# The second gate of a transformer layer: multiplied into the weights w2, or into the products

## The chip, the cores and the metric

The kernel runs on one core of a Trainium2 chip. The core has a matrix engine (PE, with its weight loads as PEld), a vector engine (DVE), a scalar engine (ACT), a general engine (POOL) and a queue (SP) that issues the transfers. Each engine takes its instructions strictly in the order of the program; an instruction whose operands aren't ready holds everything behind it on the same engine. The metric is the device time of one execution in microseconds. Before the change three runs took 2816.18, 2817.00 and 2820.16 us, with a median of 2817.0 us.

## What is computed

One layer of a transformer over 2048 rows of 1024 numbers: a retention and an attention branch, their output projection, and a feed-forward part, with a norm at the end. The part that matters here is the end of the layer:

```python
mod = (c_act @ w_mod + b_mod)[:, None, :]
sh1, sc1, g1, sh2, sc2, g2 = jnp.split(mod, 6, axis=-1)
...
x = x + g1 * (jnp.concatenate([ret, att], axis=-1) @ w_out)
h2 = _modulate(_rmsnorm(x, norm2_g), sh2, sc2)
x = x + g2 * _sqrelu_mlp(h2, w_ff1, w_ff2)       # square(relu(h @ w1)) @ w2
return _rmsnorm(x, final_norm_g)
```

`g2` is one row of 1024 numbers, so that `g2 * (u @ w2)` equals `u @ (w2 * g2)`: the gate may be put into the product or into the columns of w2.

## The kernel before

**Products of seven.** Both feed-forward matrix products are done by a scheme of Strassen's kind: two by two blocks, seven products instead of eight. Every operand is written as a sum of two 16-bit parts (high and low); a product is 12 matmuls of 128x128 by 128x512 (high-high, high-low, low-high, for four blocks of 128). Seven linear forms are built of each operand (four additions on POOL for the sums, the high part on ACT, the low part on DVE), and the seven products are added together as they come out of PSUM (DVE, with one copy on ACT).

**The up half** computes `u = square(relu(h @ w1))` in 224 products. Blocks of 256 columns of w1 are taken one after the other (an item); the first eight and the last eight items serve one half of the rows, the eight between them both halves. A product's result is added into others on DVE (L1849), goes through ReLU on ACT (L1853) and a square on POOL (L1854), and is stored. Beside it, w2 is prepared for the down half: `w2_forms` makes the seven forms of one block of 256 rows of w2. `seven` fetches two tiles of 128x1024 (`b`), builds four sums on POOL (L1891, `bs`), scales and rounds to the high part on ACT (L1896) and makes the low part on DVE (L1902, `w2f`); the results are stored (L1942, `wf`). The sixteen blocks start 7 products apart, from the first item with two halves on.

**The down half** computes `u @ w2` in 32 pairs of row tiles of 7 products each: four rounds (a quarter of the 4096 each) of eight pairs. `down` issues the 12 matmuls, `down_out` takes the product out of PSUM (L2066, tiles `d`), and `gate` multiplies the finished quarter by the gate's row (L2094, on POOL, tile `g2b`) and adds it to the row of x (L2096, tile `y`, half on POOL, half on DVE). After rounds 0 to 2 the row is stored and read again in the next round (`x1`). In the last round ACT squares it for the norm (L2106), `ending` makes the root (L1338, L1339 on POOL) and the normed row (L2121 on DVE), which is stored. In the very last pair DVE does the gate and the addition for the second half of the columns.

**Scales.** So that 16-bit parts don't overflow, powers of two are worked out once, early (`ff_scales`): `scw` for w2, `scu` for u. What is left of these scales is multiplied into the gate's row there, which is stored as `gs`; `open_late` reads it back, spread over all partitions, as `g2b`.

**What sets the order.** Steps are numbered by product. Functions are put into lists with `on(step, phase, fn, ...)`; for each step the phases run in the order

```python
FPHASES = ("pe", "sum", "hi", "lo", "relu", "out", "square", "late", "dma")
```

and each function issues its instructions. So the program's order on an engine follows from step, phase and the order of the calls of `on`. Rings of buffers (`Ring`) hold several pairs at once: eight PSUM banks, nine tiles `w` for the 16-bit forms, eight rows `y`.

## Time and profile before

| | |
|---|---|
| median of the runs | 2817.0 us |
| profiled execution | 2816.61 us |
| its span (first to last instruction) | 2814.7 us |
| PE busy | 2668.3 us (95%) |
| DVE busy | 2190.4 us (78%) |
| POOL busy | 1933.2 us (69%) |
| ACT busy | 1465.0 us (52%) |
| granted clock of PE | 0.989 |
| up half, first to last matmul of it | 1630 to 2212 us |
| down half | 2212.5 to 2794.8 us |

A row of the profile's groups reads: line of the kernel, engine, operation, what is written from what is read, shapes and number of instructions, then busy time and mean duration in ns, then the idle time of the engine just before these instructions with what ended it. In a table of stretches, each row gives the busy time of the engines between two moments. In a timeline, each row is start, duration, engine, line and operation, with the wait before it in brackets. Rows of one line or tile give least, median and greatest duration in ns. The ends of matmuls are modelled: they follow each other faster than the duration that each is given.

### The profile page before, as it was taken

The numbers are of one execution on the slowest core, as the hardware profiler recorded it, in microseconds if no ns is written. First come the engines' busy times: TensorE is split into PE (matmuls) and PEld (weight loads), VectorE is DVE, ScalarE is ACT, GpSimd is POOL, SyncE is SP. The second block draws the span as 40 slices with busy tenths as digits, with TensorE's granted clock in tenths as the row PEclk, the third lists the DMA queues.
The fourth block names the chain that finished last, engine by engine and source line by source line (L and its number), as shares of the span: only waits on it lengthen the run. The fifth ranks groups of instructions, "written<-read, shape, count | busy, mean of one in ns | idle before, by whom it ended". The sixth has DMA issues, their size and how long they took to land.

```text
span 2814.7 us, 46065 instructions
## 1 busy us (share of the span) xinstructions
PE 2668.3 (95%) x16756; PEld 1602.8 (57%) x16756; DVE 2190.4 (78%) x3126; ACT 1465.0 (52%) x2441; POOL 1933.2 (69%) x1499
## 2 busy tenths in 40 slices
PE   6998999997899999999999899999999999999996
PEld 3877788875566566555666544444444444444443
DVE  3678847777977787877877578898876688888898
ACT  2535443335777777777777745555544322222232
POOL 2527427434766668886766679988865688888887
PEclk9999999999999999999999999999999999999998
DMA  6776876855211223333121264777783757575543
GB/s 213 269 260 203 283 274 218 283 180 184 66 52 52 66 72 106 96 105 91 60 82 45 91 236 138 234 252 248 245 275 106 249 180 284 176 274 171 187 143 112
DMA packets 329778, 482.88 MB, mean 172 GB/s; under 512 B 81991, under 2 KB 192839, under 8 KB 325070
## 3 DMA queue, kind: packets, MB, share of 16 engines
q1 hardware_dynamic: 329166, 479.66, 51.7%
q8 instruction: 132, 2.16, 0.3%
q14 instruction: 96, 0.79, 0.1%
q10 hardware_dynamic: 384, 0.26, 0.0%
HBM read 327.64 MB, written 152.20 MB: 170 GB/s over the span
## 4 chain that ended last, share of the span: by engine, by line
PE 57%; DVE 6%; POOL 5%; issue 2%; DMA 2%; ACT 1%; SPq 0%; POOLq 0%; DVEq 0%; ACTq 0%
PE pu L1838 7%; PE pu L1839 7%; PE pu L1837 7%; PE pd L2056 5%; PE pd L2054 5%; PE pd L2055 5%; PE o L243 3%; PE st L210 3%; PE st L209 3%; PE mp L172 3%; PE o L242 2%; PE bank L1603 2%; PE bank L1605 2%; PE bank L1604 2%; POOL plo L226 1%
## 5 line engine op out<-in xcount | busy, mean ns | idle before, releaser
L185 DVE TENSOR_REDUCE nm<-mp 128x1 f32<-128x512 f32 (+1 forms) x576 | 390.1, 684 | 170.9 <-PE mp L172 144.7
L226 POOL TENSOR_TENSOR plo<-p,phi 128x1024 f16<-128x1024 f32 x160 | 354.1, 2214 | 175.3 <-ACT phi L219 148.0
L215 ACT ACTIVATE p<-st 128x512 f32<-128x512 f32 x576 | 338.5, 597 | 196.8 <-PE st L210 128.2
L2056 PE MATMUL pd<-w,uf 128*128 128x512 f16 x896 | 339.6, 379 | 1.2 <-DVE uf L2047 1.2
L1837 PE MATMUL pu<-hf,w1f 128*128 128x512 f16 x896 | 339.6, 379 | 0.0
L1838 PE MATMUL pu<-hf,w1f 128*128 128x512 f16 x896 | 339.6, 379 | 0.0
L1839 PE MATMUL pu<-hf,w1f 128*128 128x512 f16 x896 | 339.6, 379 | 0.0
L2054 PE MATMUL pd<-w,uf 128*128 128x512 f16 x896 | 339.6, 379 | 0.0
L2055 PE MATMUL pd<-w,uf 128*128 128x512 f16 x896 | 339.6, 379 | 0.0
L219 ACT ACTIVATE phi<-p 128x1024 f16<-128x1024 f32 x288 | 303.9, 1055 | 0.0
L1065 PE MATMUL pso<-whi,hlo_l 128*128 128x512 f32 (+1 forms) x768 | 288.5, 376 | 10.6 <-DVE hlo_l L492 10.5
L1063 PE MATMUL pso<-whi,hhi_l 128*128 128x512 f32 (+1 forms) x768 | 297.5, 387 | 0.8 <-ACT whi L512 0.8
L1064 PE MATMUL pso<-wlo,hhi_l 128*128 128x512 f32 (+1 forms) x768 | 286.8, 373 | 0.8 <-DVE wlo L516 0.8
L242 PE MATMUL o<-wv,plo 128*128 128x65 f16 x2304 | 234.7, 193 | 25.2 <-POOL plo L226 18.4
L228 DVE TENSOR_TENSOR plo<-p,phi 128x512 f16<-128x512 f32 x256 | 241.2, 943 | 19.5 <-ACT phi L219 14.4
L2094 POOL TENSOR_TENSOR d<-d,g2b 128x512 f32<-128x512 f32 x126 | 199.8, 1586 | 70.5 <-DVE d L2066 68.6
L242 PEld LDWEIGHTS <-plo 128*128 128x128 f16 x2304 | 206.3, 98 | 68.6 <-POOL plo L226 26.4
L243 PE MATMUL o<-wv,phi 128*128 128x129 f16 x2304 | 242.5, 220 | 0.0
L1854 POOL TENSOR_TENSOR r<-r 128x512 f32<-128x512 f32 x128 | 172.1, 1350 | 86.4 <-ACT r L1853 86.1
L209 PE MATMUL st<-qr,ks 128*128 128x512 f16 x576 | 220.6, 383 | 7.0 <-ACT p L215 6.6
L210 PE MATMUL st<-qr,ks 128*128 128x512 f16 x576 | 220.7, 383 | 0.4
L172 PE MATMUL mp<-ks,qr 128*128 128x512 f16 x512 | 196.8, 384 | 25.6 <-DVE nm L185 25.2
(330 smaller groups left out, 6249.1 us busy)
## 6 DMA issues: line engine op xcount, KB each, us to landing
wm<-in_w_ff SPq DMA_DIRECT2D x64, 512.0 KB, 6.9
u<-r SPq DMA_DIRECT2D x128, 256.0 KB, 4.6
ur<-u SPq DMA_DIRECT2D x128, 256.0 KB, 5.9
y<-x SPq DMA_DIRECT2D x64, 512.0 KB, 6.4
wst<-in_w_in SPq DMA_DIRECT2D x60, 512.0 KB, 6.8
wf<-w2f SPq DMA_DIRECT2D x112, 256.0 KB, 3.9
w<-wf SPq DMA_DIRECT2D x28, 1024.0 KB, 10.1
w1r<-in_w_ff SPq DMA_DIRECT2D x48, 512.0 KB, 5.3
```

The lines of the kernel that those rows point to most:

```text
L185: nc.vector.tensor_reduce(dst, src, axis=AX.X, op=ALU.max, negate=True)
L210: mm(ps, ks2[:, self.g, k], q[:, 1], start=False, stop=True)
L215: nc.scalar.activation(self.p[kt // 2][:, kt % 2], self.s.pop(kt), AF.Exp, scale=HD**-0.5)
L226: nc.gpsimd.tensor_tensor(lo, p, hi, op=ALU.subtract)
L242: mm(o[:, : HD + 1], lo[:, i, c], v[:, : HD + 1], start=False, stop=False)
L243: mm(o, hi[:, i, c], v[:, :VW], start=False, stop=last)
L1837: mm(pu[hf, i], whi, hi, start=k == 0, stop=False)
L1838: mm(pu[hf, i], whi, lo, start=False, stop=False)
L1839: mm(pu[hf, i], wlo, hi, start=False, stop=k == 3)
L2054: mm(ps, u[:, 0, b], w[:, b, 0], start=b == 0, stop=False)
L2055: mm(ps, u[:, 0, b], w[:, b, 1], start=False, stop=False)
L2056: mm(ps, u[:, 1, b], w[:, b, 0], start=False, stop=b == 3)
```

## The change

The gate is multiplied into w2 where its forms are made: each of the two fetched tiles of a block is multiplied in place by the gate's row, one tile on POOL two steps ahead of the block's first sum, the other on DVE one step ahead of it. Blocks start 8 products apart instead of 7, the fifteenth 18 after the fourteenth and the sixteenth 11 after that one. The scale of w2 takes the greatest value of the gate into account, and the row of the gate is used unscaled (no `gs`). What is left of the scales is a column `scy`.

In the down half a product is multiplied by `scy` and added in one instruction on DVE, either to a known sum (tiles `d`) or straight into the row `y`; POOL adds the known sums to the row. Multiplications by the gate are gone, and so is the special case of the last pair. The final norm's row is scaled once by the root of 1024, so that the two sums of squares are added in the same POOL instruction that adds epsilon. The row is stored two steps earlier, the ending begins three steps earlier.

```diff
+                gm = b[:, 8:9]
+                nc.vector.tensor_reduce(gm, x["g", 1], axis=AX.X, op=ALU.max, apply_absolute_value=True)
+                nc.vector.tensor_tensor(w2, w2, gm, op=ALU.mult)
...
-                g, t = x["g", 1], b[:, 8:9]
-                nc.vector.tensor_tensor(t, c, c, op=ALU.mult)
-                nc.vector.tensor_scalar_mul(t, t, 2.0**-24)
-                nc.vector.tensor_scalar(g, g, t, w2, op0=ALU.mult, op1=ALU.mult)
-                do(s + 5, "store", lambda: nc.sync.dma_start(gs_d.unsqueeze(0), g[:1]))
+                nc.vector.tensor_tensor(scy, c, c, op=ALU.mult)
+                nc.vector.scalar_tensor_tensor(scy, scy, 2.0**-24, w2, op0=ALU.mult, op1=ALU.mult)
...
-        nc.sync.dma_start(ff["g2"], gs_d.partition_broadcast(P))
+        nc.sync.dma_start(ff["g2"], gate_d[1].partition_broadcast(P))
...
+        def gated(g):
+            w, eng = x["raw", g], nc.vector if g else nc.gpsimd
+            eng.tensor_tensor(w, w, ff["g2"], op=ALU.mult)
...
             on(b0 - 5 + g, "dma", fetch, g)
+            if gate:
+                on(b0 - 2 + g, "lo" if g else "sum", gated, g)
...
+        on(20, "late", lambda: nc.scalar.activation(ff["fg"], ff["fg"], AF.Copy, scale=float(D) ** 0.5))
...
-            w2_forms(first1 + 1 + 7 * m, b)
+            w2_forms(first1 + 1 + (8 * m if m < 14 else 11 * m - 32), b)
...
+        def plus(to, x):
+            nc.vector.scalar_tensor_tensor(to, ps, scy, x, op0=ALU.mult, op1=ALU.add)
...
+        def known(k, g, n, x):
+            d = xs_[x]
+            on(at + k, "square", lambda: nc.gpsimd.tensor_tensor(y[g, n], y[g, n], d, op=ALU.add))
...
         elif i == 1:
-            gate(at, p, 0, 0, add("x"))
+            plus(y[0, 0], y[0, 0])
+            known(1, 0, 0, "x")
+            made(at + 1, p, 0, 0)
         elif i == 2:
-            xs_["u2"] = add("x")
+            plus(new("u2"), xs_["x"])
+            known(1, 0, 1, "u2")
         elif i == 3:
-            xs_["u3"] = add("u2")
+            plus(new("u3"), xs_["u2"])
+            known(1, 1, 1, "u3")
         elif i == 4:
-            gate(at, p, 1, 0, add("u3"))
+            plus(y[1, 0], y[1, 0])
+            known(0, 1, 0, "u3")
+            made(at + 1, p, 1, 0)
         elif i == 5:
-            gate(at, p, 1, 1, add("u3", xs_["u3"]))
-            add("u2", xs_["u2"])
+            plus(y[1, 1], y[1, 1])
+            plus(y[0, 1], y[0, 1])
+            made(at, p, 1, 1)
         elif i == 6:
-            gate(at, p, 0, 1, add("u2", xs_["u2"]))
+            plus(y[0, 1], y[0, 1])
+            made(at, p, 0, 1)
...
-        on(at + 1, "square", lambda: eng.tensor_tensor(c, c, ff["g2"][:, s], op=ALU.mult))
-        eng2 = nc.vector if n or fast else nc.gpsimd
-        on(at + 2, "lo" if eng2 is nc.vector else "square", lambda: eng2.tensor_tensor(y, y, c, op=ALU.add))
...
-                on(at + 4, "dma", lambda: nc.sync.dma_start(x1_d[tiles_of(p)[g]], ys.pop((p, g))))
+                on(at + 2, "dma", lambda: nc.sync.dma_start(x1_d[tiles_of(p)[g]], ys.pop((p, g))))
...
+        def root():
+            nc.gpsimd.tensor_scalar(v, ss[:, :1], ss[:, 1:], D * EPS, op0=ALU.add, op1=ALU.add)
+            nc.gpsimd.tensor_tensor(r, v, half[:, :1], op=ALU.pow)
```

The order on the engines shows it at three places. The first is POOL in the middle of the up half, around one block of w2 (`b` the fetched tiles, `bs` their sums, `w1s` the sums of w1, `r` the squares of the up products). Before:

```order
L1891 TENSOR_TENSOR bs_23826<-b_23724 128x512
L1854 TENSOR_TENSOR r_23788<-r_23788 128x512
L1891 TENSOR_TENSOR bs_23850<-b_23747,bs_23826 128x512
L1854 TENSOR_TENSOR r_23810<-r_23810 128x512
L1808 TENSOR_TENSOR w1s_23875<-w1r_23646,w1r_23648 128x512
L1891 TENSOR_TENSOR b_23724<-b_23747,b_23724 128x512
```

After:

```order
L1892 TENSOR_TENSOR b_24102<-b_24102,g2b_20946 128x1024
L1854 TENSOR_TENSOR r_24124<-r_24124 128x512
L1808 TENSOR_TENSOR w1s_24188<-w1r_23964,w1r_23966 128x512
L1854 TENSOR_TENSOR r_24147<-r_24147 128x512
L1896 TENSOR_TENSOR bs_24212<-b_24102 128x512
L1854 TENSOR_TENSOR r_24171<-r_24171 128x512
```

One instruction of 128x1024 on the gate's row (`g2b`) stands ahead of the block's first sum, with squares and a sum of w1 between them.

The second is POOL in the last round of the down half, about one pair (`us` and `ur` are the sums and parts of u for the next pair). Before:

```order
L2039 TENSOR_TENSOR us_30788<-ur_30700,ur_30702 128x512
L2094 TENSOR_TENSOR d_30670<-d_30670,g2b_20946 128x512
L2039 TENSOR_TENSOR us_30813<-us_30788,ur_30729 128x512
L2039 TENSOR_TENSOR ur_30700<-ur_30729,ur_30700 128x512
L2094 TENSOR_TENSOR d_30821<-d_30821,g2b_20946 128x512
L1338 TENSOR_SCALAR cv_e_30841<-ss_30794 128x1
L1339 TENSOR_TENSOR cy_e_30842<-cv_e_30841,half_65 128x1
L2096 TENSOR_TENSOR y_30727<-y_30727,d_30821 128x512
```

After:

```order
L2048 TENSOR_TENSOR us_30651<-ur_30561,ur_30563 128x512
L2134 TENSOR_SCALAR cv_e_30659<-ss_30555 128x1
L2135 TENSOR_TENSOR cy_e_30660<-cv_e_30659,half_65 128x1
L2048 TENSOR_TENSOR us_30678<-us_30651,ur_30588 128x512
L2048 TENSOR_TENSOR ur_30561<-ur_30588,ur_30561 128x512
L2083 TENSOR_TENSOR y_30586<-y_30586,d_30661 128x512
L2083 TENSOR_TENSOR y_30586<-y_30586,d_30702 128x512
L2048 TENSOR_TENSOR us_30678<-ur_30590,us_30678 128x512
```

The gate's multiplications are gone, the root (`cv_e`, `cy_e`) of the pair before stands ahead of the second sum, and the known sums `d` go straight into the row `y`.

The third is DVE at the end of the program, from the last low part on. Before:

```order
L2066 TENSOR_TENSOR d_31154<-pd_31138,d_31135 128x512
L2114 TENSOR_TENSOR ss_31132<-ss_31132 128x1
L2066 TENSOR_TENSOR d_31174<-pd_31156,d_31135 128x512
L2114 TENSOR_TENSOR ss_31068<-ss_31068 128x1
L2121 SCALAR_TENSOR_TENSOR y_30927<-y_30927,cy_e_31171,fgb_20948 128x1024
L2066 TENSOR_TENSOR d_31196<-pd_31179,d_31174 128x512
L2121 SCALAR_TENSOR_TENSOR y_30902<-y_30902,cy_e_31194,fgb_20948 128x1024
L2066 TENSOR_TENSOR d_31218<-pd_31201,d_31196 128x512
```

After:

```order
L2140 SCALAR_TENSOR_TENSOR y_30777<-y_30777,cy_e_30960,fgb_20948 128x1024
L2140 SCALAR_TENSOR_TENSOR y_30753<-y_30753,cy_e_30982,fgb_20948 128x1024
L2075 SCALAR_TENSOR_TENSOR y_30916<-pd_30987,scy_273,y_30916 128x512
L2075 SCALAR_TENSOR_TENSOR d_31015<-pd_31002,scy_273,d_30983 128x512
L2075 SCALAR_TENSOR_TENSOR d_31035<-pd_31019,scy_273,d_31015 128x512
L2075 SCALAR_TENSOR_TENSOR y_30936<-pd_31039,scy_273,y_30936 128x512
```

The norm of the pair before (the rows that write `y` from `cy_e`) stood on both sides of the addition for product 3 of the last pair (the third L2066 row) and now stands ahead of its first multiply-add.

More of the change, by code (lines that the diff above doesn't have):

```diff
@@ L1877, in store_u, with seven @@
         nc.sync.dma_start(dst, r.rearrange("p (q t) -> p q t", q=4))
-    def seven(b0, source, tiles, low, kinds, scale=None):
+    def seven(b0, source, tiles, low, kinds, scale=None, gate=None):
         x = {}
@@ L1944, in w2_forms @@
             scw,
+            True,
         )
@@ L2062, in down_out, with new @@
         ps = pu.pop(i)
-        def add(x, to=None):
-            to = to if to is not None else ff["r"].tile([P, 512], F32, "d")
-            nc.vector.tensor_tensor(to, ps, xs_[x], op=ALU.add)
-            return to
+        y = {(g, n): ys[p, g][:, n * 512 : (n + 1) * 512] for g in range(2) if (p, g) in ys for n in range(2)}
+        def plus(to, x):
+            nc.vector.scalar_tensor_tensor(to, ps, scy, x, op0=ALU.mult, op1=ALU.add)
+        def new(x):
+            xs_[x] = ff["r"].tile([P, 512], F32, "d")
+            return xs_[x]
@@ L2106, in square @@
             nc.scalar.activation(junk, y, AF.Square, accum_out=sums[p, g][:, n : n + 1])
[L2108 removed]
+        on(at + 1, "relu", square)
         if n == 1:
[L2110 removed]
+            on(at + 1, "relu", ending, at + 1, p, g)
     def ending(at, p, g):
         ss, y, t = sums.pop((p, g)), ys.pop((p, g)), tiles_of(p)[g]
[L2114 to L2118 removed]
+        v, r = (sm.tile([P, 1], F32, name=f"c{x}_e", tag=f"c{x}_e") for x in "vy")
+        def root():
+            nc.gpsimd.tensor_scalar(v, ss[:, :1], ss[:, 1:], D * EPS, op0=ALU.add, op1=ALU.add)
+            nc.gpsimd.tensor_tensor(r, v, half[:, :1], op=ALU.pow)
+        on(at, "square", root)
         def whole(c):
```

20 lines of the change are left out of this document (5 added, 15 removed).

## The prediction

> **What bounds the kernel now.** I read the table of busy time by stage first, with stretches cut at the borders of the two feed-forward halves: up (1630 to 2212 us) and down (from 2212.5 us).
>
> ```profile
> core 0: us, PE busy (x) PEld busy (x) DVE busy (x) ACT busy (x) POOL busy (x), PEclk, DMA share, GB/s
> 1690.00:1780.00 90.00, 90.00 (x419) 40.83 (x418) 77.09 (x84) 47.48 (x77) 90.00 (x62) 1.00 0.48 144
> 1953.70:1989.95 36.25, 36.25 (x169) 16.44 (x168) 31.48 (x36) 19.97 (x30) 29.27 (x20) 1.00 0.76 247
> ...
> 2212.50:2670.00 457.50, 457.50 (x2121) 207.42 (x2120) 377.78 (x402) 124.54 (x208) 395.35 (x253) 1.00 0.65 223
> 2670.00:2794.80 124.80, 123.54 (x570) 55.34 (x568) 117.81 (x124) 43.84 (x97) 108.52 (x83) 1.00 0.37 127
> 2794.80:2814.70 19.90, 0.00 (x0) 0.00 (x0) 14.19 (x20) 3.26 (x10) 9.76 (x12) 0.60 0.28 106
> ```
>
> PE has no idle time in either half until the last 125 us, and its clock is 1.00. So nothing that only relieves DVE or POOL can shorten these stretches. A product is 12 matmuls; 168 of them (14 products) take the 36.25 us of the second row, so a matmul goes out every 0.215 us and a product takes 2.59 us. What is left to win is the 19.90 us after the last matmul, and the 1.26 us that PE lacks in the row above. What is left to lose is PE's cover in the up half, where the change puts work.
>
> Then the timeline of the end, of PE, of DVE and of POOL, each alone:
>
> ```profile
> 2783.86 0.39 PE L2056 MATMUL pd<-w,uf 128*128 128x512 f16 x1 [0.53 <-DVE uf L2047]
> ...
> 2787.27 0.39 PE L2056 MATMUL pd<-w,uf 128*128 128x512 f16 x1 [0.64 <-DVE uf L2047]
> ```
>
> ```profile
> 2799.28 0.68 DVE L2066 TENSOR_TENSOR d<-pd,d 128x512 f32<-128x512 f32 x1
> 2800.08 1.28 DVE L2121 SCALAR_TENSOR_TENSOR y<-y,cy_e,fgb 128x1024 f32<-128x1024 f32 x1
> 2801.28 2.87 DVE L2066 TENSOR_TENSOR d<-pd,d 128x512 f32<-128x512 f32 x4
> ...
> 2806.56 0.69 DVE L2096 TENSOR_TENSOR y<-y,d 128x512 f32<-128x512 f32 x1
> ...
> 2810.13 1.42 DVE L2121 SCALAR_TENSOR_TENSOR y<-y,cy_e,fgb 128x512 f32<-128x512 f32 x2 [0.44 <-POOL cy_e L1339]
> ```
>
> ```profile
> 2807.41 0.19 POOL L1338 TENSOR_SCALAR cv_e<-ss 128x1 f32<-128x1 f32 x1 [2.76 <-DVE ss L2114]
> 2807.69 0.55 POOL L1339 TENSOR_TENSOR cy_e<-cv_e,half 128x1 f32<-128x1 f32 x1
> 2808.35 0.72 POOL L1338 TENSOR_SCALAR cv_e<-ss 128x1 f32<-128x1 f32 x1
> 2809.16 0.94 POOL L1339 TENSOR_TENSOR cy_e<-cv_e,half 128x1 f32<-128x1 f32 x1
> ```
>
> PE waits twice, 0.53 and 0.64 us, for a low part (uf) that DVE makes late; each wait hides another 0.38 - 0.215 us under the end that the matmul before it is given, so 1.5 us together. After the last matmul, at 2794.8, five additions out of PSUM (L2066) are still to come, the first of them for product 3 of the last pair of tiles, whose matmuls ended three products, 7.8 us, before that: it starts 12.3 us late. So DVE carries a backlog, and the end is this backlog and then the chain behind its last piece (gate, add, square, root, norm, store). A DVE that is 12 us late has cost PE 1.5 us: I use 10 to 12 us as the lag that the buffers absorb.
>
> **The change, part by part.** The rows of before that carry the prices:
>
> ```profile
> L2094 POOL TENSOR_TENSOR d<-d,g2b 128x512 f32<-128x512 f32 x126 | 199.8, 1586 | 70.5 <-DVE d L2066 68.6 <-DVE ss L2114 1.8
> L2096 DVE TENSOR_TENSOR y<-y,d 128x512 f32<-128x512 f32 x64 | 108.8, 1701 | 7.1 <-POOL d L2094 7.0
> L2096 POOL TENSOR_TENSOR y<-y,d 128x512 f32<-128x512 f32 x64 | 93.0, 1454 | 4.5
> ```
>
> ```profile
> L1610 DVE SCALAR_TENSOR_TENSOR xr<-bank,sco,xr x32: 734/749/752, 791.7 to 1635.7; 128x512 f32<-128x512 f32 x32
> ```
>
> ```profile
> b<-in_w_ff SPq DMA_DIRECT2D x32, 512.0 KB, 5.2
> ```
>
> *Down half, per pair of tiles (7 products, 18.1 us).* Removed are four gate multiplications (4 x 1.586 = 6.3 us) and two additions (2.9 us) on POOL, and two additions on DVE (3.4 us). Added are four additions on POOL, 1.26 us (alone, the fastest of L2094's kind) to 1.72 us each: 5.0 to 6.9 us. The seven additions from PSUM become multiply-adds; L1610 is the same form (PSUM, a column, a row), so 0.749 instead of 0.68 us, 0.5 us per pair. The first row of the stage gives 457.5 / 18.1 = 25.3 pairs, so 14.9 us of DVE and 15.6 us of POOL per pair before; after it DVE has 14.9 - 3.4 + 0.5 = 12.0 and POOL 15.6 - 9.2 + 5.0 to 6.9 = 11.4 to 13.3. All of this lies beside a PE that is already full: worth nothing by itself. In the last eight pairs, where the norm is added, DVE stands at 117.81 and POOL at 108.52 of 124.80 (17.1 and 15.7 us per pair) and work falls behind; the same subtraction leaves about 14 and 11.5 to 13.5 of 18.1. So the backlog goes, and with it the PE stalls: **-1.5 us**, if what gates PE next (POOL's sums, ACT's high parts) holds six products ahead as in the order. The norm loses its own small addition on DVE (ss) and runs a step or more earlier; the output stores move forward with it in SP's queue, past the reads of the next rows. Two waits are new. DVE's multiply-add for product 5 (and those of 5 and 6 into the first row) wait for POOL's additions of the known part: POOL gets to the one for product 5 after product 3 is out and has 5.2 us until product 5 ends, against at most 1.72 + 1.72 us for a sum ahead of it and itself. Behind that wait on DVE stand low parts that PE needs 5 products (13 us) later. And product 1 now needs its row of x, where before its first use was the add two steps later: fetched four steps (10.4 us) ahead, and a fetch of 512 KB, its size, lands in 5.2 us in the row above.
>
> *The end.* From the end of before's last addition, 2806.56 + 0.69 = 2807.25, to the end of the span at 2814.70 are 7.45 us: square on ACT, the ss addition, two POOL steps, two halves of the norm, their stores. Without the ss addition about 7.2. The last matmul is then followed by one multiply-add of 0.75 us and this chain: 0.05 + 0.75 + 7.2 = 8.0 us instead of 19.9: **-11.9 us**. Lower end 7.1, if POOL's two steps don't meet DVE (0.72 and 0.94 us there, 0.19 and 0.55 for the root before it: -0.9); upper end 9.4, if the norm of the other row (1.42 us) still stands ahead on DVE. I take 8.0, since the last rows of the order are the same.
>
> *The scales,* once, near 626 us.
>
> ```profile
> L914 DVE TENSOR_REDUCE fsb<-fg 128x1 f32<-128x1024 f32 x1 | 1.2, 1220 | 0.0
> ```
>
> A greatest value over the gate comes, of the same form as this row, and the scaling of that row of 1024 (L908) and its store go: between 0 (hidden, or the one for the other) and +1.2 us on DVE. I take **+0.5**, since two instructions over the same row stand against each other. The scaling of the final norm's row on ACT (1024 elements, once, with ACT half idle) and the column in ACT's copy are covered by PE.
>
> *Up half: the gate on w2.* Each of 16 blocks gets two multiplications of 128x1024, one on POOL, one on DVE, and blocks come 8 products apart instead of 7. Prices of the rows:
>
> ```profile
> L226 POOL TENSOR_TENSOR plo<-p,phi x160: 2114/2132/2692, 662.3 to 1607.4; 128x1024 f16<-128x1024 f32 x160
> ```
>
> ```profile
> L2121 DVE SCALAR_TENSOR_TENSOR y<-y,cy_e,fgb x18: 746/1272/2286, 2677.8 to 2810.8; 128x1024 f32<-128x1024 f32 x14, 128x512 f32<-128x512 f32 x4
> ```
>
> ```profile
> L1891 POOL TENSOR_TENSOR bs<-b,bs 128x512 f32<-128x512 f32 x4 | 5.5, 1384 | 2.5 <-DVE w2f L1902 1.9 <-DMA u<-r 0.6
> L1891 POOL TENSOR_TENSOR b<-b 128x512 f32<-128x512 f32 x2 | 3.4, 1720 | 0.0
> ```
>
> ```profile
> L1902 DVE SCALAR_TENSOR_TENSOR w2f<-b,scw,w2f 128x512 f16<-128x512 f32 x8 | 9.5, 1186 | 0.0
> L1849 DVE TENSOR_TENSOR r<-pu,r 128x512 f32<-128x512 f32 x14 | 9.4, 685 | 4.8 <-PE pu L1839 4.1 <-issue 0.6
> L1902 DVE SCALAR_TENSOR_TENSOR w2f<-bs,scw,w2f 128x512 f16<-128x512 f32 x7 | 9.4, 1347 | 0.0
> ```
>
> So 2.13 to 2.69 us on POOL and 1.27 to 2.29 us on DVE, the ends alone and meeting the other engine. The last two fences are of 1953.70 to 1989.95 us, two blocks in 14 products. POOL: 29.27 us, 12.3 of them w2 sums (5.5, 3.4, and two more of the kind at 3.4), so 17.0 for the rest, which follows the products. Over 16 products (41.4 us) that is 17.0 x 16/14 + 12.3 + 4.3 to 5.4 = 36.0 to 37.1 us, 87 to 90% (81% before). DVE: 31.48 us, the w2 low parts 18.9 less some 0.08 us of overlap each, 17.7 for 15 of them; the rest 13.8 grows to 15.8, 14 low parts are 16.5, the gates 2.5 to 4.6: 34.8 to 36.9 us, 84 to 89% (87% before). The wider spacing pays for the gates. Nothing of it is on PE's path as long as DVE and POOL are not later than those 10 us; 1690 to 1780 us, with POOL busy 90.00 of 90.00 us and PE too, shows that a full POOL is borne for 35 products. I cost it at **nothing**; its cover is PE's two halves of work, and if the engines overrun, each microsecond past 10 to 12 us of lag is one of PE. The gates also wait for the block's fetch, three steps (7.8 us) after its issue instead of five; it lands in 5.2 us, so they need not wait; a late one would hold POOL's squares and DVE's PSUM additions, who have the same 10 us. The last two blocks, at 175 and 186 of 220 steps, fall among products with one half each, where DVE and POOL had most room.
>
> *Sum:* -1.5 - 11.9 + 0.5 = **-12.9 us**. The profiled execution was 2816.6 us (span 2814.7, 1.9 around it), 0.4 below the median of 2817.0; against the median I forecast **2804.1 us**, 2801.5 to 2806 by the ends of the tail and the scatter of the runs.
>
> **A price for meeting engines.** How far POOL and DVE slow each other when both run from SBUF decides the up half:
>
> ```profile
> L2047 DVE TENSOR_TENSOR uf<-ur,uf x128: 670/681/1757, 2196.7 to 2786.5; 128x512 f16<-128x512 f32 x128
> ```
>
> ```profile
> 1966.36 1.72 POOL L1891 TENSOR_TENSOR bs<-b,bs 128x512 f32<-128x512 f32 x1
> 1968.04 1.72 POOL L1891 TENSOR_TENSOR b<-b 128x512 f32<-128x512 f32 x1
> ...
> 1978.73 1.04 POOL L1854 TENSOR_TENSOR r<-r 128x512 f32<-128x512 f32 x1 [4.14 <-ACT r L1853]
> 1979.73 1.27 POOL L1891 TENSOR_TENSOR bs<-b,bs 128x512 f32<-128x512 f32 x1
> ```
>
> Alone a square takes 1.04 and a sum 1.27 us; in a row against a busy DVE two sums come 1.68 us apart, 0.4 us more, less than the 0.67 us that a DVE low part needs alone. A strict taking of turns would add 0.67. The Trainium skill ("SBUF — State Buffer", Who interferes with whom) says that a DVE instruction with two SBUF inputs and a GpSimd instruction that reads SBUF lock each other out for the whole instruction, and that one with a single SBUF input doesn't contend. By that the multiply-adds from PSUM are harmless (L1610's 734 to 752 ns agree), and the up half would be overfull, the rival below; the trace shows 0.4 where the rule gives 0.67.
>
> **Rivals.**
> *Slower: strict turns in the up half.* Counting every POOL instruction and every two-input DVE instruction one after the other, a block of 8 products asks for 4.57 squares x 1.04 + 6.29 sums x 1.27 + 2.13 = 14.9 us of POOL and 11 x 0.67 + 1.2 = 8.6 of DVE, 23.5 of 20.7 us. Fourteen blocks fall 39 us behind; less 12 borne, PE loses 27 us: 2817 - 13 + 27 = 2831. It decides from 1.8 us of overrun per block. Against it: the same count of before is 18.8 of 18.1 us, yet DVE waited 4.1 us for PE in that stretch. 10%.
> *The turns as measured:* with 0.4 us per meeting a POOL instruction adds only its time alone less 0.27 us to DVE's 0.67 (0.77 for a square, 1.0 for a sum, 2.0 for the gate at 2.69 - 0.67): 3.5 + 6.3 + 2.0 + 8.6 = 20.4 of 20.7, just full. With 1 to 1.3 us more per block, fourteen blocks lag 14 to 18 us, and PE loses 2 to 8 us: 2806 to 2812. 12%.
> *The backlog stays.* If the product-5 wait makes DVE and POOL hand lateness to each other in the last pairs, PE's end stays and half of the tail with it: 2809 to 2817. 8%. For it speaks that DVE waited for POOL at L2096 already (7.0 us); against it, the 1.8 us of slack above (5.2 less 3.4).
>
> **Numbers.** The forecast has 70%. Times within 0.2% (5.6 us, about what a measurement of this kernel tells from no change) are 2811.4 to 2822.6. Faster: 70 + 12 + 1 = 83%; same 6%; slower 11%. The range of 8 in 10 runs from 2801 (shortest tail, and the scatter of the runs) to 2811.
>
> **What would show it.** Right: after the last matmul about 8 us instead of 19.9, with one multiply-add between it and the last square; no PE row with a wait for uf in the last pairs; DVE and POOL at about 12 us per pair in the down half, with the multiply-adds at 0.75 us; PE still at 100% from 1780 to 2070 us with DVE and POOL below 92%. Wrong: waits of PE for w1f or PSUM between 1780 and 2150 us, gates on POOL far over 2.7 us, or DVE waiting long for POOL's known part.

## The result, and the profile after

The changed kernel takes 2810.8 us (median of 13 runs, 2807.0 to 2816.5) against 2818.4 us of the kernel before in the same sessions (2816.2 to 2820.3): a ratio of 0.9975, 95% interval 0.9968 to 0.9983. It is faster by about 7.6 us, or a quarter of a per cent, where 12.9 us were forecast. The time lies above the forecast (2804.1) and above the 2801.5 to 2806 us given with it, at the upper end of the wider range (2801 to 2811).

The profiled execution of the changed kernel took 2814.1 us, 3.3 above the median, with a span of 2812.3 us. The first view to read is where its two halves lie: the row of the first of the up half's three matmul lines, with its first and last start. Before:

```profile
L1837 PE MATMUL pu<-hf,w1f x896: 379/379/379, 1630.1 to 2212.0; 128*128 128x512 f16 x180
```

After:

```profile
L1837 PE MATMUL pu<-hf,w1f x896: 376/379/379, 1633.0 to 2223.9; 128*128 128x512 f16 x180
```

The up half starts 2.9 us later. That is scatter and no effect of the change: the profiled executions of all eleven kernels of this study start it between 1627.6 and 1635.2 us. From its first to its last matmul the up half took 581.9 us before and takes 590.9 now, **9.0 us more**. From there to the end of the span it was 2814.7 - 2212.0 = 602.7 us and is 2812.3 - 2223.9 = 588.4, **14.3 us less**. The three add up: 2.9 + 9.0 - 14.3 = -2.4 us, the difference of the spans.

The stretches by stage, of the changed kernel, answer to the first table of the prediction (the last row lies behind the last matmul, which is now given an end at 2804.9):

```profile
core 0: us, PE busy (x) PEld busy (x) DVE busy (x) ACT busy (x) POOL busy (x), PEclk, DMA share, GB/s
1690.00:1780.00 90.00, 90.00 (x419) 40.83 (x418) 77.09 (x82) 49.64 (x81) 90.00 (x62) 1.00 0.49 146
1953.70:1989.95 36.25, 36.25 (x170) 16.41 (x169) 36.25 (x33) 17.49 (x29) 32.17 (x21) 1.00 0.60 197
...
2212.50:2670.00 457.50, 457.50 (x2121) 207.39 (x2120) 273.92 (x354) 125.36 (x208) 301.03 (x202) 1.00 0.63 224
2670.00:2794.80 124.80, 124.80 (x580) 56.57 (x579) 98.65 (x109) 50.73 (x107) 102.75 (x81) 1.00 0.45 152
2804.90:2812.30 7.40, 0.00 (x0) 0.00 (x0) 3.49 (x5) 0.72 (x2) 1.25 (x3) 0.70 0.38 142
```

In the down half DVE fell from 377.78 to 273.92 us and POOL from 395.35 to 301.03 of 457.5. PE lacks nothing in the last pairs (124.80 of 124.80, before 123.54), and 7.4 us instead of 19.9 follow the last matmul. In the up half DVE is now busy without a gap (36.25 of 36.25, before 31.48). The end on DVE, from its timeline:

```profile
2802.41 1.41 DVE L2075 SCALAR_TENSOR_TENSOR y<-pd,scy,y 128x512 f32<-128x512 f32 x2 [1.91 <-PE pd L2065]
2804.93 0.75 DVE L2075 SCALAR_TENSOR_TENSOR y<-pd,scy,y 128x512 f32<-128x512 f32 x1 [1.11 <-PE pd L2065]
2805.59 1.41 DVE L2140 SCALAR_TENSOR_TENSOR y<-y,cy_e,fgb 128x512 f32<-128x512 f32 x2
2807.85 1.41 DVE L2140 SCALAR_TENSOR_TENSOR y<-y,cy_e,fgb 128x512 f32<-128x512 f32 x2 [0.85 <-POOL cy_e L2135]
```

DVE waits for PE ahead of each multiply-add: no backlog is left, and one multiply-add stands behind the last matmul. The other row's norm (2805.59) still stands ahead of the last one, but it fills the gap while the last row is squared, and DVE waits another 0.85 us after it.

The loss lies in the up half. The waits of PE from 1660 to 2240 us, of which before had none:

```profile
PE pu L1839 <- DVE w1f L1819: 4.4, 8, 1.4
PE pu L1837 <- DVE r L1849: 1.8, 2, 1.6
```

PE waits for what DVE makes: low parts of w1, and the addition that frees a PSUM bank. These waits are 6.2 of the 9.0 us; the rest is later starts that the modelled ends of the matmuls hide, some 0.16 us at each wait, and gaps too small to be listed. Where they lie, two stretches of the changed kernel show (columns as above):

```profile
1780.00:2080.00 300.00, 298.17 (x1382) 134.99 (x1381) 289.59 (x275) 148.51 (x230) 264.02 (x165) 1.00 0.66 212
2080.00:2220.00 140.00, 135.35 (x619) 59.40 (x618) 127.35 (x134) 72.04 (x113) 115.33 (x77) 1.00 0.73 235
```

How late DVE is shows in two timelines. PE's last matmul of product 149 (products are numbered here from the fifth of the up half on), and DVE some 17 us later, when it gets to that product (the second of the two additions at 2051.35):

```profile
2034.54 0.38 PE L1839 MATMUL pu<-hf,w1f 128*128 128x512 f16 x1
```

```profile
2042.46 2.64 DVE L1907 SCALAR_TENSOR_TENSOR w2f<-b,scw,w2f 128x512 f16<-128x512 f32 x1
2045.02 1.27 DVE L1849 TENSOR_TENSOR r<-pu,r 128x512 f32<-128x512 f32 x2
2046.22 1.56 DVE L1819 SCALAR_TENSOR_TENSOR w1f<-w1s,sc,w1f 128x512 f16<-128x512 f32 x1
2047.70 1.52 DVE L1907 SCALAR_TENSOR_TENSOR w2f<-bs,scw,w2f 128x512 f16<-128x512 f32 x1
2049.15 2.28 DVE L1892 TENSOR_TENSOR b<-b,g2b 128x1024 f32<-128x1024 f32 x1
2051.35 1.28 DVE L1849 TENSOR_TENSOR r<-pu,r 128x512 f32<-128x512 f32 x2
```

DVE never waits here, and its instructions fall into two kinds: the additions out of PSUM (L1849) take 1.27 us for two in a row, 0.68 each, and everything that reads two operands from SBUF (L1907, L1819, L1892) takes 1.5 to 2.6 us. Measured in this way, from the end of a product to DVE's start on it, DVE's lag is 2.0 us at product 54, 10.9 at 102, 17.0 at 149: 15.0 us in 95 products, about 1.3 us per block of 8. A block therefore asks for about 20.7 + 1.3 = 22.0 us. The groups by shape between 1780 and 2080 us, before and after, show where it comes from. Before:

```profile
L1849 DVE TENSOR_TENSOR r<-pu,r 128x512 f32<-128x512 f32 x115 | 77.3, 683 | 31.0 <-PE pu L1839 22.1 <-DMA u<-r 5.3 <-issue 3.2
L1902 DVE SCALAR_TENSOR_TENSOR w2f<-b,scw,w2f 128x512 f16<-128x512 f32 x64 | 75.4, 1178 | 1.5 <-ACT w2f L1896 1.5
L1902 DVE SCALAR_TENSOR_TENSOR w2f<-bs,scw,w2f 128x512 f16<-128x512 f32 x48 | 66.6, 1387 | 0.0
L1819 DVE SCALAR_TENSOR_TENSOR w1f<-w1r,sc,w1f 128x512 f16<-128x512 f32 x25 | 31.7, 1268 | 0.8 <-ACT w1f L1813 0.8
L1819 DVE SCALAR_TENSOR_TENSOR w1f<-w1s,sc,w1f 128x512 f16<-128x512 f32 x35 | 30.9, 883 | 0.0
```

After:

```profile
L1854 POOL TENSOR_TENSOR r<-r 128x512 f32<-128x512 f32 x63 | 92.2, 1463 | 8.7 <-ACT r L1853 8.6
L1907 DVE SCALAR_TENSOR_TENSOR w2f<-b,scw,w2f 128x512 f16<-128x512 f32 x54 | 82.3, 1530 | 0.0
L1849 DVE TENSOR_TENSOR r<-pu,r 128x512 f32<-128x512 f32 x111 | 73.0, 677 | 4.3 <-DMA u<-r 4.3
L1907 DVE SCALAR_TENSOR_TENSOR w2f<-bs,scw,w2f 128x512 f16<-128x512 f32 x40 | 54.3, 1361 | 5.6 <-issue 2.8 <-ACT w2f L1901 2.8
L1819 DVE SCALAR_TENSOR_TENSOR w1f<-w1s,sc,w1f 128x512 f16<-128x512 f32 x32 | 37.2, 1162 | 0.0
L1892 POOL TENSOR_TENSOR b<-b,g2b 128x1024 f32<-128x1024 f32 x14 | 37.0, 2644 | 0.4 <-DMA b<-in_w_ff 0.4
L1819 DVE SCALAR_TENSOR_TENSOR w1f<-w1r,sc,w1f 128x512 f16<-128x512 f32 x24 | 34.1, 1421 | 0.0
L1892 DVE TENSOR_TENSOR b<-b,g2b 128x1024 f32<-128x1024 f32 x14 | 27.5, 1963 | 0.5 <-DMA b<-in_w_ff 0.5
```

The gates cost what was forecast (2.64 us on POOL, 1.96 on DVE) and hardly wait for their fetch (0.4 and 0.5 us in 300 us). But the low parts, the same instructions as before, went from 1178 to 1530 ns (of `b`), from 883 to 1162 and from 1268 to 1421 ns (of w1); only those of `bs` did not change (1387, 1361). Over all four kinds the mean rose from 1.19 to 1.39 us, some 30 us for the 150 of them in these 300 us.

What stretches a low part can be read from the same traces. Between 1640 and 2220 us of the changed kernel, 31 of the 274 low parts of w1 and w2 overlap with no instruction on POOL; each of these takes 0.73 to 0.75 us. The other 243 overlap with one and take 1.39 us on average, at most 2.88. Before, 56 and 217 low parts divide in the same way: at most 0.75 us, and 1.27 on average. The additions out of PSUM, with one operand from SBUF, take 0.68 us in both cases:

```profile
L1849 DVE TENSOR_TENSOR r<-pu,r x221: 671/677/693, 1643.1 to 2219.6; 128x512 f32<-128x512 f32 x111
L1907 DVE SCALAR_TENSOR_TENSOR w2f<-b,scw,w2f x64: 734/1523/2877, 1788.8 to 2167.0; 128x512 f16<-128x512 f32 x64
```

DVE no longer waits for PE anywhere in this stretch (22.1 us of such waits before).

### The profile page after: what moved, and what is told of

Read it like the earlier page. It is cut to its first block, busy times and chain, and to the rows that moved or that the text cites. A ratio compares the mean times of both kernels' runs of the same rounds, so it can differ in the third digit from the quotient of the medians.

```text
span 2812.3 us, 45879 instructions
## 1 busy us (share of the span) xinstructions
PE 2673.6 (95%) x16756; PEld 1605.7 (57%) x16756; DVE 2122.4 (75%) x3061; ACT 1463.5 (52%) x2442; POOL 1886.5 (67%) x1453
## 5 line engine op out<-in xcount | busy, mean ns | idle before, releaser
L226 POOL TENSOR_TENSOR plo<-p,phi 128x1024 f16<-128x1024 f32 x160 | 355.1, 2220 | 171.4 <-ACT phi L219 141.3
L1837 PE MATMUL pu<-hf,w1f 128*128 128x512 f16 x896 | 339.6, 379 | 1.8 <-DVE r L1849 1.8
L2083 POOL TENSOR_TENSOR y<-y,d 128x512 f32<-128x512 f32 x128 | 210.5, 1646 | 137.8 <-ACT uf L2052 90.8
L228 DVE TENSOR_TENSOR plo<-p,phi 128x512 f16<-128x512 f32 x256 | 239.1, 934 | 19.5 <-ACT phi L219 14.2
L243 PEld LDWEIGHTS <-phi 128*128 128x128 f16 x2304 | 205.4, 97 | 20.7
## 6 DMA issues: line engine op xcount, KB each, us to landing
w<-wf SPq DMA_DIRECT2D x28, 1024.0 KB, 10.8
```

The lines of the kernel that those rows point to most:

```text
L226: nc.gpsimd.tensor_tensor(lo, p, hi, op=ALU.subtract)
L243: mm(o, hi[:, i, c], v[:, :VW], start=False, stop=last)
L1837: mm(pu[hf, i], whi, hi, start=k == 0, stop=False)
```

## The experiments

**Theory.** POOL and DVE's instructions with two operands from SBUF hold each other up, so their times add, in full or in part: each new POOL instruction is paid once more, at least in part, on DVE. A block asks for more than its 20.7 us, DVE falls behind from block to block, and PE waits once the buffers are used up. **Rivals.** The own time of DVE (or of POOL) is what overflows; or the order of the waits around the gates makes single pieces late.

For each run the table gives the time, the ratio to before in the same session (2818.4 to 2818.8 us), the length of the up half from its first to its last matmul of L1837, and what DVE and POOL were busy of the 300 us from 1780 to 2080 us (the last four columns are of one profiled execution each).

| kernel | median us | ratio, 95% | up half us | last of it to end us | DVE | POOL |
|---|---|---|---|---|---|---|
| before | 2818.4 | | 581.9 | 602.7 | 263.7 | 243.9 |
| after | 2810.8 | 0.9975 (0.9968 to 0.9983) | 590.9 | 588.4 | 289.6 | 264.0 |
| down half alone | 2804.2 | 0.9945 (0.9933 to 0.9957) | 581.4 | 588.5 | 261.9 | 240.7 |
| both gates on DVE | 2804.7 | 0.9954 (0.9941 to 0.9966) | 584.5 | 588.4 | 295.2 | 233.4 |
| both gates on POOL | 2817.2 | 0.9994 (0.9985 to 1.0003) | 596.8 | 588.4 | 281.5 | 288.6 |
| all blocks 9 apart | 2810.1 | 0.9964 (0.9951 to 0.9978) | 586.9 | 588.4 | 283.5 | 266.1 |
| squares on ACT | 2802.0 | 0.9939 (0.9927 to 0.9952) | 581.0 | 588.4 | 247.6 | 163.9 |
| gates on DVE, 9 then 12 apart | 2803.1 | 0.9945 (0.9931 to 0.9958) | 581.1 | 588.4 | 282.2 | 227.9 |
| fetch and gates three steps earlier | 2817.6 | 0.9990 (0.9981 to 0.9999) | 593.8 | 588.4 | 288.9 | 264.7 |
| blocks 7 apart | 2828.9 | 1.0037 (1.0025 to 1.0048) | 607.6 | 588.4 | 292.4 | 273.4 |
| squares on ACT, blocks 7 apart | 2802.3 | 0.9944 (0.9924 to 0.9963) | 581.7 | 588.5 | 288.4 | 191.9 |

What comes after the up half is the same in all ten kernels that have the new down half, to 0.1 us. Everything that sets them apart happens in the up half.

**The down half alone.** The gates on w2 and their spacing are undone, so this kernel leaves the second gate out of its result:

```diff
-            if gate:
-                on(b0 - 2 + g, "lo" if g else "sum", gated, g)
...
-            w2_forms(first1 + 1 + (8 * m if m < 14 else 11 * m - 32), b)
+            w2_forms(first1 + 1 + 7 * m, b)
```

> The changed kernel without the two multiplications by the gate and with blocks of w2 7 products apart again, so that the up half is that of before and the down half and the end are those of the change; the second gate is left out of the result. All theories lay the missing half of the gain at the up half: PE then waits nowhere in the up half beyond its first products, the end takes 7.4 us as in the changed kernel, and the time is 2802 to 2804 us against 2818 before. If the down half itself is worth only half of what was forecast, it stays near 2811.

2804.2 us (2799.3 to 2805.6), at the upper edge of what was expected: 14.2 us below before, with an up half like that of before (581.4 us). So the change in the down half, its end and the scales is worth the whole forecast and a little more, and the gates on w2 take back 2810.8 - 2804.2 = 6.6 us of it.

**Both gates on DVE, both on POOL.** The two runs pull the rivals apart: one loads DVE more, the other relieves it.

```diff
-            w, eng = x["raw", g], nc.vector if g else nc.gpsimd
+            w, eng = x["raw", g], nc.vector
...
-                on(b0 - 2 + g, "lo" if g else "sum", gated, g)
+                on(b0 - 2 + g, "lo", gated, g)
```

The other kernel has `nc.gpsimd` and `"sum"` at the same places.

> Both gates of a block on DVE, otherwise the changed kernel. Theory (POOL and DVE take turns at what both need, so the sum of their times counts): a gate on DVE takes 1.2 us of the turns, on POOL 2.0 us, so a block asks for 0.8 us less; DVE falls behind by at most 0.5 us per block instead of 1.3, PE hardly waits, 2802 to 2805 us. First rival (DVE's own time is what is full, at 97%): DVE gets 1.2 to 2.1 us more per block, PE loses 17 to 29 us more, 2828 to 2840 us. Second rival (waits for the gates, by order, not load): about as the changed kernel, 2811 us.

> Both gates of a block on POOL, otherwise the changed kernel. Theory of turns: 0.8 us more per block, so about 12 us more lost by PE, 2820 to 2825 us. First rival (DVE's own time): DVE is relieved of 2.1 us per block, no PE waits, 2802 us. Second rival (order): about 2811 us.

Both gates on DVE, 1780 to 2080 us (columns as in the first table):

```profile
1780.00:2080.00 300.00, 300.00 (x1392) 136.01 (x1390) 295.24 (x295) 152.43 (x237) 233.40 (x156) 1.00 0.67 218
```

Both on POOL:

```profile
1780.00:2080.00 300.00, 293.98 (x1355) 132.30 (x1353) 281.45 (x254) 144.37 (x223) 288.63 (x174) 1.00 0.65 209
```

With DVE at 98% PE has no idle time; with DVE at 94% and POOL at 96% it loses 6 us here. The times are 2804.7 and 2817.2 us. DVE's own time is not what decides: the kernel that gives DVE more is the fastest of the three, and the one that relieves it the slowest. POOL's own time is not it either, as far as the waits show: in these 300 us of the changed kernel DVE has no wait for a result of POOL. 2804.7 us lies in the range that the theory gave; 2817.2 lies on the side expected but 2.8 us below the 2820 to 2825, so the second gate on POOL cost about half of the 12 us reckoned. A gate costs 1.77 us on DVE and 2.70 on POOL (its means in the two runs), and on POOL it also slows DVE. In the first run the lag still grew by about 0.8 us per block (2.7 us at product 54, 12.7 at 149), where at most 0.5 was expected; so my count of a block is too low there too.

**All blocks 9 apart.**

```diff
-            w2_forms(first1 + 1 + (8 * m if m < 14 else 11 * m - 32), b)
+            w2_forms(first1 + 1 + 9 * m, b)
```

> All sixteen blocks 9 products apart (the last starts two products later than in the changed kernel), gates as in the change. Theory of turns: a block's 21.5 us (22.9 with the 6.5% that the changed kernel measured above the count) fit into 23.3 us while products come in two halves, so the lag stays below 8 us up to product 164; the last three blocks then lie among products of one half, ask for 28.8 of 23.3 us and bring 16 us of lag, of which PE loses 2 to 4 us: 2804 to 2807 us. Rival (DVE's own time): the same direction, DVE busy below 95%. Rival (order of the waits): the spacing changes little, 2809 to 2811 us.

From 1780 to 2080 us and from there to 2220 us:

```profile
1780.00:2080.00 300.00, 300.00 (x1391) 135.99 (x1390) 283.49 (x278) 152.09 (x235) 266.14 (x169) 1.00 0.68 214
2080.00:2220.00 140.00, 135.38 (x623) 60.17 (x622) 129.63 (x133) 70.91 (x111) 113.80 (x75) 1.00 0.74 236
```

With 23.3 us per block the lag stays between 0 and 7 us from product 53 to 165 and PE waits for nothing, as the theory says. Then it grows to 18 us, and PE loses 4.6 us, among the last three blocks, which now fall among the products with one half each. In the prediction I had taken those for the ones with most room. They are not: such an item has 7 products instead of 14 for the same forms of w1, and 7 products give only half the time to make them. So the median is only 0.7 us below that of the change, which the runs don't tell apart (2802.5 to 2814.2 us). The time itself misses the 2804 to 2807 us expected and lies in the range of the rival on order; what speaks against that rival is the lag, which the spacing did remove up to product 165.

**The squares on ACT.** If POOL's time is paid in part a second time on DVE, taking any other work from POOL must do what taking the gates away did. The squares of the up products go to ACT; gates and spacing stay as in the change:

```diff
-            on(at + 2, "square", lambda: nc.gpsimd.tensor_tensor(r, r, r, op=ALU.mult))
+            on(at + 2, "square", lambda: nc.scalar.activation(r, r, AF.Square))
```

> The changed kernel with one edit: the squares of the up products run on ACT instead of POOL. Theory (POOL's time and that of DVE's instructions with two inputs from SBUF add up to more than 20.7 us per block of 8 products): a block loses 4.57 squares, at 0.77 us each that a square adds, so 3.5 us per block; the overrun of about 1.3 us per block is gone, DVE stays within 5 us of PE's products from 1700 to 2150 us, PE waits less than 2 us in the up half after its first products, low parts of w2 take less than 1.4 us instead of 1.53. Time 2801 to 2804. Rival (what comes late is the order of waits around the gates: POOL's gate waits for the block's fetch and holds what stands behind it): squares were not the cause, the lag stays, about 2811. Second rival: ACT, with some 20 of 36 us busy here before and 2.3 squares per block pair more at about 0.5 to 0.7 us each, becomes late itself; then PE waits for high parts, which come from ACT, and the time is above 2811.

```profile
1780.00:2080.00 300.00, 300.00 (x1392) 135.98 (x1391) 247.56 (x288) 190.81 (x309) 163.94 (x103) 1.00 0.68 223
```

And its groups by shape in these 300 us:

```profile
L1849 DVE TENSOR_TENSOR r<-pu,r 128x512 f32<-128x512 f32 x115 | 77.1, 685 | 43.2 <-PE pu L1839 35.5 <-ACT w1f L1813 4.9 <-ACT r L1854 2.6
L1907 DVE SCALAR_TENSOR_TENSOR w2f<-b,scw,w2f 128x512 f16<-128x512 f32 x56 | 71.7, 1286 | 0.0
L1819 DVE SCALAR_TENSOR_TENSOR w1f<-w1s,sc,w1f 128x512 f16<-128x512 f32 x36 | 35.7, 991 | 0.0
L1892 DVE TENSOR_TENSOR b<-b,g2b 128x1024 f32<-128x1024 f32 x14 | 17.0, 1216 | 0.0
```

2802.0 us (2800.1 to 2805.7). DVE's instructions are the same ones, and more of them fit into the 300 us (288, after: 275), yet they take 247.6 us instead of 289.6: 42 us of DVE's busy time in the changed kernel went with POOL's squares. More low parts now meet no POOL instruction (about 125 of 274 between 1640 and 2220 us, 31 in the change), and these again take 0.73 to 0.75 us. The lag is at most 5.5 us (5 expected), and DVE waits for PE again (35.5 us). ACT carries the squares at 0.61 us each and is busy 190.8 of 300, no bound. This version is faster than both kernels; its interval (0.9927 to 0.9952) lies wholly below that of the change.

Over all eleven kernels, the mean of the low parts in these 300 us goes with the share of time that POOL is busy: 1.08 us at 55% (this run), 1.18 to 1.26 at 64 to 81%, 1.35 to 1.43 at 88 to 91%, 1.56 at 96% (both gates on POOL). The DMA engines are no such measure: they were busy 77% of this stretch before, 66% after and 68% here.

**Gates on DVE, and room where the items are short.** As above with both gates on DVE, and

```diff
-            w2_forms(first1 + 1 + (8 * m if m < 14 else 11 * m - 32), b)
+            w2_forms(first1 + 1 + (9 * m if m < 12 else 12 * m - 34), b)
```

> The changed kernel with both gates on DVE and the blocks spread otherwise: the first twelve 9 products apart, the last four 12 apart, so that all of the last ones lie among the products with one half. Theory (sum of the turns): with both gates on DVE the overrun at a spacing of 8 was 0.75 us per block; a product more per block gives 2.59 us less what the other work of a product asks of it, about 0.6 us of room, so the lag stays under 5 us up to product 160, and 12 instead of 9 products in the last part keep it under 8 us there, where equal spacing of 9 with a gate on each engine rose to 17. PE waits for nothing after the first products: 2801 to 2803. Rival (DVE's own time decides): 2 x 2.6 us of gates and the low parts make DVE late as soon as its busy share passes 95%, as at 1780 to 2080 us with both gates on it at a spacing of 8: no better than that run, 2805 or more.

```profile
1780.00:2080.00 300.00, 300.00 (x1392) 136.02 (x1391) 282.17 (x290) 150.52 (x232) 227.94 (x155) 1.00 0.67 213
2080.00:2220.00 140.00, 140.00 (x650) 63.47 (x649) 136.88 (x141) 75.20 (x118) 111.81 (x76) 1.00 0.77 251
```

2803.1 us (2801 to 2803 expected), and PE waits for nothing. The lag was to stay under 5 us up to product 160 and under 8 behind it; it is at most 5.3 from product 53 to 165, and then it grows to 12 us. PE does not notice, with DVE busy 136.88 of 140 us. The time is 1.6 us below that of both gates on DVE with the spacing of the change, which the runs don't tell apart; the 1.6 us that PE lost there from 2080 to 2220 us are gone in the trace.

**Fetch and gates three steps earlier.** The order of the waits is the suspect here; the work is the same.

```diff
-            on(b0 - 5 + g, "dma", fetch, g)
+            on(b0 - (8 if gate else 5) + g, "dma", fetch, g)
...
-                on(b0 - 2 + g, "lo" if g else "sum", gated, g)
+                on(b0 - 5 + g, "lo" if g else "sum", gated, g)
```

> The changed kernel with the fetches of w2's blocks and the two gates three steps earlier, spacing and engines as in the change. Theory (sum of the turns): the same work in the same time, so the lag grows by about 1.3 us per block as before: 2808 to 2813. Rival (order of waits: the gate follows the fetch too closely and holds POOL's squares and DVE's PSUM additions behind it): the lag stays under 5 us and PE waits for nothing in the up half: 2801 to 2804.

2817.6 us (2810.9 to 2820.0), by the medians 6.8 us above the change and 4.6 above the range that I gave for the theory; the two intervals just touch, and in the profiled executions the up half is only 2.9 us longer. That rival falls in the form in which it was put, since the earlier gates bring nothing; but the theory does not say why they do harm. DVE and POOL are as busy as in the change (288.9 and 264.7 of 300 us). The gate on DVE takes 2.53 us instead of 1.96 and one kind of sum on POOL 1.62 instead of 1.42, but the low parts of `b` take less, 1.34 instead of 1.53. So the order changes who meets whom, and it may have a price of its own. Which meeting it is was not found.

**Blocks 7 apart.** What is the wider spacing worth?

```diff
-            w2_forms(first1 + 1 + (8 * m if m < 14 else 11 * m - 32), b)
+            w2_forms(first1 + 1 + 7 * m, b)
```

> The changed kernel with the blocks 7 products apart throughout, as in the kernel before; the gates stay. Theory (sum of the turns): a block has 18.1 us instead of 20.7 and one product's worth of other work less, so it overruns by about 2.5 to 3 us instead of 1.3; sixteen blocks make 40 to 48 us, less some 15 that the buffers absorb: PE loses 25 to 33 us in the up half instead of 9, 2826 to 2836. Rival (the spacing does nothing, the lag is one of waits around single blocks): 2808 to 2816.

2828.9 us, slower than before and within the 2826 to 2836 expected; the up half takes 25.7 us more than before. From product 100 on the lag doesn't grow any more (15 to 21 us) and PE waits instead, in a pattern that comes back every two blocks. PE's timeline has these waits at the same place of two such rounds:

```profile
1957.38 0.38 PE L1837 MATMUL pu<-hf,w1f 128*128 128x512 f16 x1 [1.97 <-DVE r L1849]
...
1997.60 0.38 PE L1837 MATMUL pu<-hf,w1f 128*128 128x512 f16 x1 [1.97 <-DVE r L1849]
```

40.2 us for two blocks, 20.1 for one, whose 7 products give PE 18.1 us of work. This is the plainest measure of what a block asks for: 20.1 us with 7 products beside it, 22.0 with 8 (above). The overrun is thus 2.0 us per block, less than the 2.5 to 3 expected.

**Squares on ACT, blocks 7 apart.** Both edits at once.

> The changed kernel with both edits at once: the up squares on ACT and the blocks of w2 7 products apart throughout; the gates stay. With squares on POOL this spacing gave 2828.9 us and PE waits of about 25 us in the up half. Theory (turns of POOL and of DVE's two-input instructions): four squares per block of 7 products are gone from POOL, and the measured relief from them was 42 us of DVE's busy time and 100 of POOL's in 300 us at a spacing of 8, which is far over the 2.7 us per block of overrun: lag under 6 us, PE waits under 2 us in the up half, 2801 to 2805. Rival (a spacing of 7 is too short in itself, since the fetches, the stores and ACT's high parts of w2 come in less time, with ACT now carrying the squares too): PE waits stay at 10 us or more, over 2810.

```profile
1780.00:2080.00 300.00, 300.00 (x1392) 135.98 (x1391) 288.36 (x301) 196.09 (x320) 191.89 (x112) 1.00 0.74 235
```

2802.3 us. The spacing that cost 26 us of PE with the squares on POOL costs nothing without them. The lag stands at 5 to 8 us (under 6 was expected) and doesn't grow. So with less work on POOL no wider spacing was needed.

## Why the prediction was right and wrong

*The stalls in the last pairs, -1.5 us: right.* PE has no idle time there.

*The end, -11.9 us: right, and a little short.* It fell from 19.9 to 7.4 us, -12.5; I had 8.0, with 7.1 and 9.4 as ends. The other row's norm, the reason given for 9.4, does stand ahead on DVE, but it fits into a wait. Together with the stalls the part behind the up half became 14.3 us shorter against 13.4 forecast.

*The waits that the new order adds in the down half: right, they cost nothing.* DVE at 273.92 / 25.3 = 10.8 us per pair against 12.0, POOL at 301.03 / 25.3 = 11.9 against 11.4 to 13.3. DVE is lower because its low parts became faster, which I had held fixed. From 2212.5 to 2670 us, before and then after:

```profile
L2047 DVE TENSOR_TENSOR uf<-us,uf 128x512 f16<-128x512 f32 x76 | 102.8, 1353 | 0.0
L2047 DVE TENSOR_TENSOR uf<-ur,uf 128x512 f16<-128x512 f32 x101 | 95.7, 947 | 2.9 <-ACT uf L2043 2.9
```

```profile
L2075 DVE SCALAR_TENSOR_TENSOR y<-pd,scy,y 128x512 f32<-128x512 f32 x121 | 88.3, 747 | 108.8 <-PE pd L2065 108.8
L2056 DVE TENSOR_TENSOR uf<-ur,uf 128x512 f16<-128x512 f32 x101 | 80.8, 800 | 8.6 <-ACT uf L2052 8.6
L2056 DVE TENSOR_TENSOR uf<-us,uf 128x512 f16<-128x512 f32 x76 | 79.7, 1048 | 0.0
```

The same mechanism, with the other sign: with less on POOL, 1353 became 1048 ns and 947 became 800. The multiply-adds take 747 ns, as L1610 had said (749). In the last eight pairs DVE has 98.65 / 6.9 = 14.3 us per pair (about 14 forecast), POOL 14.9 (11.5 to 13.5 forecast, too low).

*The scales, +0.5 us: not shown either way.* The run of the down half alone contains them and is 14.2 us faster by the medians, against 14.3 in the part behind the up half; half a microsecond is less than these runs can show (its interval is 12 to 19 us).

*The up half, costed at nothing: wrong, and this is the step that failed.* "The wider spacing pays for the gates" took the durations of before for all instructions that stay, and asked of each engine alone whether its sum fits: 87 to 90% for POOL, 84 to 89% for DVE. POOL came to 88.0% (264.0 of 300 us). DVE came to 96.5% (289.6 of 300), since its low parts were stretched, over all kinds from 1.19 to 1.39 us, by a POOL that is busy more often; those 30 us are 10% of the 300, the difference to the forecast. The step that failed is thus the price of the low parts, held at what they cost in the kernel before, and with it the cover that was counted on. The sign of being wrong that the prediction named, waits of PE for w1f or PSUM between 1780 and 2150 us, is what came. In the profiled execution of the changed kernel the up half took 9.0 us more; the medians, against the down half alone, show 6.6.

The prediction named the true case and gave it 12%: "the turns as measured", POOL's time and DVE's two-operand time counted as one budget, 20.4 of 20.7 us, with 1 to 1.3 us more if it is a little short: 2806 to 2812 us. It was 22.0 of 20.7, the 1.3 us of that rival, and 2810.8 us lies in its range. That the time fits so well is in part luck: the rival reckoned with the lag of fourteen blocks alone, but the lag had come down to 10 us at product 173, and the larger part of PE's loss comes with the last two blocks, which the prediction took for easy (below). What the prediction set against a full budget, 4.1 us of waits of DVE for PE in that stretch of before, showed room in a kernel without the gates, not room for them.

How far the engines lock each other out was the open price. By full turns a block asks for 23.5 us, by the 0.4 us per meeting of one quoted place for 20.4; the measured 22.0 lies between. The 0.67 us that both counts give a low part alone was read from the down half (L2047); a low part of the up half that meets no POOL instruction takes 0.74, so full turns come to about 24.2 us (11 x 0.07 more). From that sum a meeting cost about 0.55 us (an estimate: 2.2 us less for some 12 POOL instructions, so 0.74 - 0.18). The Trainium skill ("SBUF — State Buffer", Who interferes with whom) has the full lock for a DVE instruction with two SBUF inputs against a GpSimd instruction that reads SBUF, and, outside DVE's 2-port modes, none for one with a single SBUF input. Its second half agrees wherever these runs can show it (L1849 at 677 to 685 ns with POOL busy from 55 to 88%). Its first half agrees in direction; counted over whole instructions, as here, it puts a block about 2 us too high (24.2 against 22.0).

*The lag that the buffers absorb, 10 to 12 us: too low.* In the changed kernel PE's first wait after the start of the up half comes at product 148, with DVE some 15 us behind; with the blocks 7 apart the lag levels off at 15 to 21 us. That is why only part of the 16 blocks' 20 us of overrun reached PE.

*The last two blocks, "where DVE and POOL had most room": wrong.* At 2080 to 2220 us PE is busy 135.35 of 140 us in the changed kernel, the larger part of its loss; DVE's lag, at 10 us around product 173, rises there to 18.7 at 193.

## What to carry to other kernels

Where POOL and DVE both run from SBUF, add the times of POOL's instructions and of DVE's instructions with two SBUF operands into one sum per step, at their undisturbed durations, and compare that sum with the step; two engines at 81 and 87% can be one budget that is nearly full. Take the sum as an upper bound: here it came to about 24.2 us for a block that asked for 22.0, and in the kernel before it was over the step already (18.8 of 18.1 us by the prediction's count) while DVE still had waits for PE. Moving work to an engine outside that pair then relieves both: the squares on ACT gave 2802.0 us, and 2802.3 at the old spacing. Both gates on DVE with more room came to 2803.1 us, which the runs don't tell apart from it. Read from the engine's own idle column whether a buffer still covers it: in each kernel here in which DVE had next to no wait for PE left in the 300 us, it was falling behind or already 15 us and more late, some 90 products before PE showed it in the changed kernel. With 4.8 us of such waits left (squares on ACT, blocks 7 apart), at 96% busy, it was not.

## What was not expected of the hardware

Taking the squares (92.2 us of POOL in 300) off POOL freed 42 us on DVE, without touching one of DVE's instructions. A low part on DVE takes 0.74 us when no POOL instruction runs beside it, and up to 2.88 us when one does; an addition out of PSUM takes 0.68 us in both cases. The same multiplication of 128x1024 takes 1.22 us on DVE beside a half-idle POOL, 1.96 in the change and 2.53 with the gates three steps earlier; on POOL it took 2.63 us even with the squares gone. And the same work in another order (fetch and gates earlier) was 6.8 us slower by the medians, with nearly the same busy times on both engines; the cause stays open.
